# A two-layer encoder's feed-forward layer: weight sums by accumulating DMAs, a new order of seven products, and PSUM banks exchanged between two products

## Chip, cores and metric

The kernel runs on one core of a Trainium2 chip. The metric is the device time of one execution in microseconds (us). Shown are the median of three runs, and one profiled execution.

## What is computed

The reference is an encoder trunk with 1024 tokens of width 1024 and two layers. Each layer is a token mixer (latent attention in layer 0, differential attention in layer 1) and a gated feed-forward part, with a norm before and after each. The change lies in the feed-forward part alone:

```python
def conv_ffn(x, w_up, conv_w, conv_b, w_down):
    u = x @ w_up                                   # 1024 -> 2 * 2816
    c = conv_b
    for j in range(3):                             # width 3, along the tokens
        c = c + conv_w[j] * up[:, j:j + s]         # up: u padded by one token at both ends
    g, val = c[..., :2816], c[..., 2816:]
    return (gelu(g) * val) @ w_down                # 2816 -> 1024

h = h + rms_norm(conv_ffn(rms_norm(h, norm_g[i, 2]), ...), norm_g[i, 3])
```

## The kernel before, in words

All is fp32. Each operand of a matmul is split in a high part (rounded, by ScalarE, `split`, line 185) and the rest (a subtraction on VectorE, line 186); three matmuls (`mm3`, lines 176 and below) make one product of full precision. Both products of the feed-forward part are done by Strassen-Winograd: a 2x2 partition with seven block products in place of eight, at the cost of sums of operands and results.

**First product** (`Sums`, lines 882 to 935). HID = 2816 gives NC = 22 blocks n of 128 hidden columns, each with a gate and a value part. A block has seven products of 12 matmuls (128x128 by 128x512), named for their operands: `ae`, `bg`, `su`, `cd`, `ac`, `sh`, `dg`. They run in three PSUM accumulators: x (`ae`, then `bg` on top), y (`su`, then `ac`, then `dg` on top), z (`cd`, then `sh` on top). Between two products on one accumulator VectorE or ScalarE reads it: after `su` an add and a copy, after `ac` a copy and `add(q3, z, q3)`, after `sh` `add(q1, z, q1)` (line 931). y and z are the two halves of one two-bank PSUM tile (`big`, two buffers); x is a one-bank tile (`pv` or `pj` in turn). The loop over the blocks (lines 1081 to 1124) runs `ae(n)`, `su(n)`, `sh(n-1)`, `dg(n-1)`, `cd(n)`, `bg(n)`, `ac(n)`; the first four blocks have their `ae` and `bg` done ahead, so there the loop has five products. The weights and their sums come from SyncE's and GpSimd's DMA queues; two of the sums are made by accumulating DMAs (lines 856 and 857). `hidden` does the convolution and the gating, `left` the sums of the left operands of the second product, which go to DRAM (`sl_d`).

**Second product** (lines 973 to 1214). The 22 hidden blocks make G = 11 pairs g. With A, B the even and odd block for tokens 0 to 511, C, D those for tokens 512 to 1023, and e, f, g, h the quarters of the pair's rows of w_down, the seven products are, in order: A e; S4 h; B g; S1 (f - e); D (g - h + f - e); S2 (h - f + e); S3 (h - f). Each product is 11 operands times 4 token tiles times 3 matmuls of 512 columns, and accumulates in four PSUM banks: alternately `lone_banks` (the one-bank tiles pv, t, t, pj) and `pairs_of_banks` (two `big` tiles). S3 adds onto the banks of S2.

- `operands` (line 1006) splits, for each g, the left operand (loaded from `sl_d` in chunks of four g, `load_sr`, two buffers) and the right one, into a ring of five wide slots (`pairs`); the last product's eleven operands go to slots of their own (`drop=True`) and its matmuls run token tile by token tile.
- `load_q` (line 987) loads e by SyncE's queue and h, g, f by GpSimd's, one product ahead of use. The sums f - e and so on are subtractions on VectorE (`u`, lines 1031 and 349), in place in `raw[g]`, a wide slot of four quarters per pair.
- SBUF has 20 wide slots (2048 floats a partition) and 15 narrow ones.
- `finish_tile(t)` adds the residual and the norm for 128 tokens: tiles 0 to 3 behind S2, tiles 4 to 7 each behind its part of S3. In layer 0 `put` turns each tile for the next layer, and `ahead` loads and splits that layer's first weights (partly on GpSimd).

The instructions are put in order for each engine by a planner that models times; priorities follow the order of the program. DMAs stamped with one token (`then`, line 980) keep their order on GpSimd's queue. Waits between engines are derived from the tiles that are read and written. Each engine's queue runs in order.

Of the kernel before, what the change touches and what calls it, by code (L numbers as in the profile page):

```python
# [120 lines left out]
def hybrid_encoder_kernel(  # L121
# [697 lines left out]
    def ffn(i, aT, rest, first, res_ap, dst_ap, ahead):  # L819
# [8 lines left out]

        cw = cp.tile([P, 2 * NC * 4], F32, name="cw", tag="cw")
        nc.sync.dma_start(out=cw, in_=conv[i])  # L830

        taps = cw[:, NC * 4 :].rearrange("p (b j) -> p b j", j=4)[:, :, :3]
        nc.vector.tensor_scalar(out=taps, in0=taps, scalar1=-1.0, scalar2=None, op0=ALU.mult)
# [48 lines left out]
        class Sums:  # L882
# [16 lines left out]
            def ae(self, w):  # L899
                self.x = small(("pv", "pj")[self.n % 2])  # L900
                product(self.x, w, 0, "e")
                copy(self.m1, self.x)
# [5 lines left out]
            def open(self, w):  # L908
                if self.parked:
                    self.place()  # L910
                    copy(self.q[0], self.parked[1])
                self.w = w
                o = big()
                self.y, self.z = o[:, :512], o[:, 512:]
# [6 lines left out]
            def cd(self):  # L921
                product(self.z, self.w["s"], 0, "e-f")
# [51 lines left out]
        A, B_, S1, S2, S3, S4, D_ = 6, 4, 0, 1, 2, 3, 5  # L974
        E, F, G_, H = 0, 1, 2, 3
# [11 lines left out]
        def load_q(g, q):  # L987
            if g == len(raw):
                raw.append(ar.alloc(2048))
            src = w_down[i, 2 * g + q // 2][:, (q % 2) * 512 : (q % 2 + 1) * 512]  # L990
            if q == E:
                nc.sync.dma_start(out=rq(g, q), in_=src)
            else:
                then(nc.gpsimd.dma_start(out=rq(g, q), in_=src))  # L994

        def load_sr(at, g, n):
            sr = r_sr.next()
            then(
                nc.gpsimd.dma_start(  # L999
                    out=sr.f[:, : n * 512].rearrange("p (g t) -> p g t", g=n),  # L1000
                    in_=sl_d[g : g + n, :, at * 512 : (at + 1) * 512].rearrange("g p t -> p g t"),
                )
            )
            return sr

        def operands(at, right, ahead=None, drop=False, last=None, loaded=()):
# [5 lines left out]
            sr, loaded = None, list(loaded)  # L1012
            for g in range(G):
                if ahead is not None:
                    load_q(g, ahead)
                if last and g == G - 1:
                    src = last()
                else:
                    if g % 4 == 0:
                        sr = loaded.pop(0) if loaded else load_sr(at, g, min(4, G - g - (last is not None)))  # L1020
                    src = sr.f[:, (g % 4) * 512 : (g % 4 + 1) * 512]
# [4 lines left out]
                split(right(g), *w.cols(512, 512))  # L1026
# [3 lines left out]

        def u(g, op, a, b, q):
            op(rq(g, q), rq(g, a), rq(g, b))
            return rq(g, q)
# [26 lines left out]
        for m in range(2):  # L1060
            for n in range(2):
                sums[2 * m + n].ae(w1[2 * m + n])
# [18 lines left out]
        for n in range(NC):  # L1081
# [8 lines left out]
            if end:  # L1090
                aT.free("u")
                for g in range(2):
                    load_q(g, E)
# [7 lines left out]
            if n + 1 < NC:  # L1101
                nxt = weights(n + 1)
            cur.cd()
            if end:
                aT.free("e-f")
                for g in range(2, 4):
                    load_q(g, E)
            if n >= 4:
                cur.bg(w["ab"])
            if n == NC - 2:  # L1110
# [3 lines left out]
                loaded = [load_sr(A, 4 * j, 4) for j in range(2)]  # L1114
            if end:
                aT.free("g")
                for g in range(4, 6):
                    load_q(g, E)
            else:
                weights_late(nxt)  # L1120
            cur.ac()
            if end:
                aT.free("h-f")
            old, w = cur, nxt
# [4 lines left out]
        xb = lone_banks()  # L1129
        for g in times(xb, operands(A, lambda g: rq(g, E), H, False, lambda: hid[0][:, :512], loaded)):  # L1130
            if g == 1:
                cur.sh()
                aT.free("h")
                for g2 in range(6, G - 1):
                    load_q(g2, E)
            elif g == 3:
                cur.dg()
                aT.free("-u-g")
                load_q(G - 1, E)
# [8 lines left out]
        yb = pairs_of_banks()  # L1148
        product2(yb, operands(S4, lambda g: rq(g, H), G_))
# [4 lines left out]
        product2(xb, operands(B_, lambda g: rq(g, G_), F), True)  # L1154
# [4 lines left out]
        product2(yb, operands(S1, lambda g: u(g, sub, F, E, E)), True)  # L1159
# [38 lines left out]
        ops = list(operands(S3, lambda g: u(g, sub, H, F, E), drop=True))  # L1198
# [340 lines left out]
```

## Time and profile before

| | |
|---|---|
| median of 3 runs | 2652.86 us (2648.47 to 2655.63) |
| the profiled execution | 2651.43 us, of which its span from first to last instruction is 2649.7 us |
| TensorE busy | 2552.2 us, 96%; mean granted clock 0.988 of full speed |
| VectorE busy | 1958.5 us, 74% |
| ScalarE busy | 1341.4 us, 51% |
| GpSimd busy | 366.3 us, 14% |
| DMA | 313.33 MB, mean 118 GB/s |

PE is TensorE's matmul row and PEld its weight loads, DVE is VectorE, ACT ScalarE, POOL GpSimd, SP SyncE. A time in square brackets behind a group is the idle time of the engine just before it, with what ended it. The first layer's feed-forward products lie at about 600 to 1040 us (first) and 1037 to 1264 us (second), the second layer's at about 2000 to 2420 and 2418 to 2641 us.

### The profile page before, as it was taken

How to read it: one execution, taken by the hardware profiler on the slowest of the kernel's cores; microseconds unless marked ns; L12 is line 12 of the kernel's file. 1: busy time of each engine (PE TensorE's matmuls, PEld its weight loads, DVE VectorE, ACT ScalarE, POOL GpSimd, SP SyncE). 2: the span in 40 equal slices, each digit the busy share in tenths (PEclk: the TensorE clock that was granted, in tenths of full speed). 3: DMA queues.
4: the chain of work that ended last, by engine and by line, in shares of the span. 5: the costliest groups of instructions: out<-in, count | busy, mean ns of one | idle time of the engine just before them, and what ended most of it. 6: DMA issues, size and time to landing. Idle time of an engine off the chain costs nothing. (4 is left out here: it accounts for less than half of the span.)

```text
span 2649.7 us, 34107 instructions
## 1 busy us (share of the span) xinstructions
PE 2552.2 (96%) x12720; PEld 2124.2 (80%) x12720; DVE 1958.5 (74%) x3085; ACT 1341.4 (51%) x2411; POOL 366.3 (14%) x464
## 2 busy tenths in 40 slices
PE   8999999998999999999799999998998999999998
PEld 7888888786788888887588888887786888888886
DVE  6776666566877777678578787788677877777677
ACT  5454455445545545445355555566445554555444
POOL 0000001101111112200322222223001111112200
PEclk9999999999999999999899999999999999999999
DMA  4211102235445545633533222323235554546534
GB/s 157 67 43 40 36 32 85 80 131 155 147 133 146 151 143 180 225 122 112 155 80 80 65 71 70 80 64 120 102 119 151 152 146 132 147 142 212 198 112 147
DMA packets 123209, 313.33 MB, mean 118 GB/s; under 512 B 13473, under 2 KB 34849, under 8 KB 120225
## 3 DMA queue, kind: packets, MB, share of 16 engines
q0 software_dynamic: 49520, 154.17, 20.9%
q1 hardware_dynamic: 60592, 148.58, 16.4%
q10 hardware_dynamic: 12928, 8.39, 1.0%
q8 instruction: 100, 1.64, 0.3%
q14 instruction: 69, 0.56, 0.1%
HBM read 216.19 MB, written 69.73 MB: 108 GB/s over the span
## 5 line engine op out<-in xcount | busy, mean ns | idle before, releaser
L176 PE MATMUL big<-a,a 128*128 128x512 f32 (+2 forms) x3696 | 886.6, 388 | 20.5 <-ACT a L185 9.2
L176 PEld LDWEIGHTS big<-a,a 128*128 128x128 f32 x3696 | 680.4, 189 | 152.8 <-ACT a L185 11.5
L176 PE MATMUL pj<-a,a 128*128 128x512 f32 x1878 | 478.8, 396 | 9.1 <-DVE b L186 6.1
L176 PEld LDWEIGHTS pj<-a,a 128*128 128x128 f32 x1878 | 344.5, 189 | 82.4 <-DVE b L186 7.5
L176 PE MATMUL big<-a,b 128*128 128x512 f32 x1296 | 366.1, 404 | 13.7 <-DMA b<-b 5.8
L176 PE MATMUL pv<-a,a 128*128 128x256 f32 (+1 forms) x2130 | 365.1, 321 | 7.3 <-DVE a L186 4.7
L176 PEld LDWEIGHTS pv<-a,a 128*128 128x128 f32 x2130 | 315.6, 196 | 47.1 <-DVE a L186 11.4
L176 PEld LDWEIGHTS big<-a,b 128*128 128x128 f32 x1296 | 236.1, 189 | 75.0 <-DVE b L352 16.9
L185 ACT ACTIVATE a<-t 128x512 fp32r<-128x512 f32 (+1 forms) x376 | 206.5, 584 | 175.2 <-PE t L242 172.9
L186 DVE TENSOR_TENSOR a<-t,a 128x512 fp32r<-128x512 f32 (+1 forms) x376 | 239.9, 665 | 51.2 <-ACT a L185 50.6
L185 ACT ACTIVATE a<-a 128x512 fp32r<-128x512 f32 x306 | 175.7, 624 | 188.6 <-PE big L176 83.1
L185 ACT ACTIVATE a<-b 128x1024 fp32r<-128x1024 f32 (+2 forms) x198 | 203.9, 1034 | 106.1 <-PE big L176 42.9
L176 PE MATMUL big<-a 128*128 128x512 f32 x1056 | 244.9, 393 | 6.5 <-DVE b L352 6.5
L186 DVE TENSOR_TENSOR a<-a,a 128x512 fp32r<-128x512 f32 x306 | 196.6, 686 | 71.2 <-ACT a L185 71.2
L176 PEld LDWEIGHTS big<-a 128*128 128x128 f32 x1056 | 199.3, 189 | 49.6 <-DVE b L352 8.1
L186 DVE TENSOR_TENSOR a<-b,a 128x1024 fp32r<-128x1024 f32 (+5 forms) x178 | 211.7, 1192 | 29.6 <-ACT a L185 29.5
L242 PE MATMUL t<-ident,b 128*128 128x128 f32 x1456 | 205.2, 276 | 25.2 <-DVE a L186 10.2
L242 PEld LDWEIGHTS t<-ident,b 128*128 128x128 f32 x1456 | 169.4, 141 | 60.6 <-DVE a L186 19.3
L1404 ACT ACTIVATE b<-b,s 128x1024 f32<-128x1024 f32 x128 | 146.8, 1149 | 103.5 <-DVE s L1393 102.4
L1393 DVE CUSTOM_DVE_ANT_0 b<-big,a 128x1024 f32<-128x1024 f32 x128 | 154.1, 1216 | 23.5 <-PE big L176 22.0
L880 ACT ACTIVATE b<-big 128x512 f32<-128x512 f32 x132 | 77.9, 590 | 161.2 <-DVE big L352 110.6
L940 DVE SCALAR_TENSOR_TENSOR b<-b,cw,b 128x1023 f32<-128x1023 f32 x88 | 112.9, 1283 | 34.2 <-ACT b L939 34.2
(148 smaller groups left out, 2656.6 us busy)
## 6 DMA issues: line engine op xcount, KB each, us to landing
b<-w_up SPq DMA_DIRECT2D x132, 256.0 KB, 2.9
a<-sl_d POOLq DMA_DIRECT2D x28, 1024.0 KB, 5.5
b<-w_up SPq DMA_DIRECT2D x52, 512.0 KB, 3.4
b<-w_up POOLq DMA_DIRECT2D x88, 256.0 KB, 4.4
sl_d<-a POOLq DMA_DIRECT2D x22, 1024.0 KB, 7.0
a<-w_down POOLq DMA_DIRECT2D x66, 256.0 KB, 5.4
b<-b POOLq DMA_DIRECT2D x64, 256.0 KB, 3.8
h_d<-b SPq DMA_DIRECT2D x24, 512.0 KB, 2.8
```

Source lines behind the costliest of these rows:

```text
L176: return nc.tensor.matmul(o, lhsT=lhsT, rhs=rhs, start=start, stop=stop, skip_group_check=more)
L185: nc.scalar.activation(hi, src, AF.Copy)
L186: (eng or nc.vector).tensor_tensor(out=lo, in0=src, in1=hi.bitcast(F32), op=ALU.subtract)
L242: nc.tensor.transpose(t[:, j, :], c, ident)
L880: nc.scalar.activation(dst, src, AF.Copy)
L940: nc.vector.scalar_tensor_tensor(out=t[:, 1:], in0=e[:, : S - 1], scalar=wc[0], in1=t[:, 1:], op0=ALU.mult, op1=ALU.add)
L1393: nc.vector.tensor_tensor_reduce(out=em.f, in0=sc, in1=dv, scale=1.0, scalar=3.0e38, op0=ALU.add, op1=ALU.min, accum_out=s8[:, m : m + 1],)
L1404: nc.scalar.activation(em.f, em.f, AF.Exp, bias=s8[:, m : m + 1], scale=-1.0, accum_out=z)
```

## The change

- First product: y gets a one-bank tile `t` (two buffers), z the tile `pj`, x the tile `pv` (in the four blocks done ahead `pv` and `pj` as before). `bg(n)` now stands before `cd(n)`.
- Second product: it starts in `pairs_of_banks` and takes turns with `lone_banks` from there. The order of the last three products is now S2, D, S3 in place of D, S2, S3, so that S2 is still in the pairs of banks that S3 adds to, but D lies between them.
- Weight sums: odd hidden blocks are stored with the opposite sign (another set of conv taps and biases is negated at the start), and the right half of the result has its sign turned by the gain, so that every sum of weights has plus signs only: e, then + f, + h, + g in place in `raw[g]`'s first quarter, and h + f in its third. Each is an accumulating DMA from w_down on GpSimd's queue (`add_q`), issued behind the split of the same g. `raw[g]` has three quarters. The 44 subtractions a layer are gone; three products take their right operand with a minus sign (`neg`: the same two instructions in other forms).
- Chunks of left operands are requested when a chunk has been used up (`load_left`), in one list over all products; the e quarters are requested a little earlier.

```diff
-        taps = cw[:, NC * 4 :].rearrange("p (b j) -> p b j", j=4)[:, :, :3]
-        nc.vector.tensor_scalar(out=taps, in0=taps, scalar1=-1.0, scalar2=None, op0=ALU.mult)
+        taps = cw[:, NC * 4 :].rearrange("p (b s j) -> p b s j", s=2, j=4)
+        for part in (taps[:, :, 0, :3], taps[:, :, 1, 3:]):
+            nc.vector.tensor_scalar(out=part, in0=part, scalar1=-1.0, scalar2=None, op0=ALU.mult)
...
-            def ae(self, w):
-                self.x = small(("pv", "pj")[self.n % 2])
+            def ae(self, w, tag="pv"):
+                self.x = small(tag)
...
-                o = big()
-                self.y, self.z = o[:, :512], o[:, 512:]
+                self.y = small("t")
...
             def cd(self):
+                self.z = small("pj")
                 product(self.z, self.w["s"], 0, "e-f")
...
-        A, B_, S1, S2, S3, S4, D_ = 6, 4, 0, 1, 2, 3, 5
-        E, F, G_, H = 0, 1, 2, 3
+        S1, S2, S3, S4, B_, D_, A = range(7)
+        E, G_, H = 0, 1, 2
...
+        def weight(g, name):
+            q = "efgh".index(name)
+            return w_down[i, 2 * g + q // 2][:, (q % 2) * 512 : (q % 2 + 1) * 512]
+
+        def load_e(g):
+            raw.append(ar.alloc(1536))
+            nc.sync.dma_start(out=rq(g, E), in_=weight(g, "e"))
+
+        def load_q(g, q, name):
+            then(nc.gpsimd.dma_start(out=rq(g, q), in_=weight(g, name)))
+
+        def add_q(g, q, name):
+            then(nc.gpsimd.dma_start(out=rq(g, q), in_=weight(g, name), accum_op=ALU.add))
...
+        chunks = [(at, g, min(4, G - g - (at == A))) for at in (A, S4, B_, S1, S2, D_, S3) for g in range(0, G, 4)]
+        def load_left():
+            if chunks:
+                at, g, n = chunks.pop(0)
+                loaded.append(r_sr.next())
...
+        def operands(q, ahead=lambda g: None, neg=False, last=None, drop=False):
             for g in range(G):
...
                 split(src, *w.cols(0, 512))
-                split(right(g), *w.cols(512, 512))
+                hi, lo = w.cols(512, 512)
+                if neg:
+                    nc.scalar.activation(hi, rq(g, q), AF.Copy, scale=-1.0)
+                    minus_sum(lo, rq(g, q), hi.bitcast(F32))
+                else:
+                    split(rq(g, q), hi, lo)
+                if g % 4 == 3 or g == G - 1:
+                    loaded.pop(0)
+                    load_left()
+                ahead(g)
...
+            if n >= 4:
+                cur.bg(w["ab"])
...
             cur.cd()
...
-            if n >= 4:
-                cur.bg(w["ab"])
...
-        xb = lone_banks()
-        for g in times(xb, operands(A, lambda g: rq(g, E), H, False, lambda: hid[0][:, :512], loaded)):
+        xb = pairs_of_banks()
+        for g in times(xb, operands(E, lambda g: load_q(g, H, "h"), last=lambda: hid[0][:, :512])):
...
-        yb = pairs_of_banks()
-        product2(yb, operands(S4, lambda g: rq(g, H), G_))
+        yb = lone_banks()
+        product2(yb, operands(H, lambda g: load_q(g, G_, "g")))
...
-        product2(xb, operands(B_, lambda g: rq(g, G_), F), True)
+        product2(xb, operands(G_, lambda g: add_q(g, E, "f"), neg=True), True)
...
-        product2(yb, operands(S1, lambda g: u(g, sub, F, E, E)), True)
+        product2(yb, operands(E, lambda g: add_q(g, E, "h"), neg=True), True)
...
         nc.sync.dma_start(out=gp, in_=norm_g[i, 3].partition_broadcast(P))
+        nc.vector.tensor_scalar(out=gp[:, 512:], in0=gp[:, 512:], scalar1=-1.0, scalar2=None, op0=ALU.mult)
...
+        xb = pairs_of_banks()
+        product2(xb, operands(E, lambda g: add_q(g, E, "g")))
+        for t in range(4):
+            add(f[t].f[:, 512:], xb[t], f[t].f[:, 512:])
         yb = lone_banks()
-
-        def g_less_u(g):
-            u(g, sub, H, E, E)
-            return u(g, sub, G_, E, G_)
-
-        product2(yb, operands(D_, g_less_u))
+        product2(yb, operands(E, lambda g: add_q(g, H, "f"), neg=True))
         for t in range(4):
             add(f[4 + t].f[:, :512], yb[t], m1v[t])
         ar.free(m1)
-        xb = pairs_of_banks()
-        product2(xb, operands(S2, lambda g: rq(g, E)))
-        for t in range(4):
-            add(f[t].f[:, 512:], xb[t], f[t].f[:, 512:])
...
-        ops = list(operands(S3, lambda g: u(g, sub, H, F, E), drop=True))
+        ops = list(operands(H, drop=True))
```

## Rows read from the trace of the kernel before

**Rows 1.** The page's busy times: engine, us, share, instructions.

```profile
PE 2552.2 (96%) x12720; PEld 2124.2 (80%) x12720; DVE 1958.5 (74%) x3085; ACT 1341.4 (51%) x2411; POOL 366.3 (14%) x464
```

**Rows 2.** Timeline of PE around S3, both layers: start, us, instructions, [idle before].

```profile
1226.43 13.02 PE L176 MATMUL big<-a 128*128 128x512 f32 x56 [1.77 <-DVE b L352]
...
1253.04 2.61 PE L176 MATMUL big<-a 128*128 128x512 f32 x7 [2.03 <-DVE b L352]
...
2607.95 16.87 PE L176 MATMUL big<-a 128*128 128x512 f32 x66 [1.78 <-DVE b L352]
2625.68 15.26 PE L176 MATMUL big<-a 128*128 128x512 f32 x66 [0.86 <-DVE b L352]
```

**Rows 3.** Timeline of PE in the first product, blocks with seven products.

```profile
706.35 2.88 PE L176 MATMUL pv<-a,a 128*128 128x512 f32 x12
709.07 2.88 PE L176 MATMUL big<-a,a 128*128 128x512 f32 x12
...
720.89 3.04 PE L176 MATMUL big<-a,b 128*128 128x512 f32 x12
...
772.21 6.51 PE L176 MATMUL big<-a,a 128*128 128x512 f32 x28
...
1009.37 3.06 PE L176 MATMUL big<-a,b 128*128 128x512 f32 x12
```

**Rows 4.** Groups of weight loads, 720.89 to 1009.37 us: count, busy, mean ns, idle before.

```profile
L176 PEld LDWEIGHTS big<-a,b 128*128 128x128 f32 x180 | 32.6, 188 | 11.0 <-DVE b L352 4.5
```

**Rows 5.** Timeline of PE at the first product's start and end.

```profile
647.83 3.01 PE L176 MATMUL big<-a,a 128*128 128x512 f32 x12 [1.94 <-DVE b L352]
652.43 1.20 PE L176 MATMUL big<-a,a 128*128 128x512 f32 x4 [1.59 <-ACT b L880]
653.81 3.06 PE L176 MATMUL big<-a,b 128*128 128x512 f32 x12 [0.18 <-DVE b L352]
...
671.05 3.02 PE L176 MATMUL big<-a,b 128*128 128x512 f32 x12 [1.30 <-DVE b L352]
...
1029.43 3.02 PE L176 MATMUL big<-a,b 128*128 128x512 f32 x12 [0.66 <-DVE b L352]
...
2035.61 4.60 PE L176 MATMUL big<-a,b 128*128 128x512 f32 x12 [0.18 <-DVE b L352]
```

**Rows 6.** Timeline of DVE at four places of the first product.

```profile
644.13 1.42 DVE L352 TENSOR_TENSOR b<-b,b 128x512 f32<-128x512 f32 x2 [4.21 <-DMA b<-w_up]
...
653.07 0.68 DVE L352 TENSOR_TENSOR b<-big,b 128x512 f32<-128x512 f32 x1
...
777.85 0.69 DVE L352 TENSOR_TENSOR b<-big,b 128x512 f32<-128x512 f32 x1 [1.95 <-PE big L176]
...
1028.70 0.68 DVE L352 TENSOR_TENSOR b<-big,b 128x512 f32<-128x512 f32 x1
```

**Rows 7.** Groups of the second product, 1074.9 to 1226.4 us: the weight sums.

```profile
L349 DVE TENSOR_TENSOR a<-a 128x512 f32<-128x512 f32 x44 | 29.9, 690 | 11.1 <-DMA a<-w_down 10.1
```

**Rows 8.** One line's instructions, duration ns min/median/max: the form that the signed split takes.

```profile
L356 DVE SCALAR_TENSOR_TENSOR b<-b,b x16: 679/682/693, 582.7 to 2013.9; 128x512 f32<-128x512 f32 x16
```

**Rows 9.** One line's instructions: an accumulating DMA on POOL, its issue and its landing.

```profile
L856 POOL DMA_DIRECT2D b<-w_up x44: 843/859/943, 617.9 to 2377.5; - x44
...
DMA to landing us min/median/max: 3.5/4.1/4.8
```

**Rows 10.** One line's instructions: issue and landing of the left operands' chunks.

```profile
L999 POOL DMA_DIRECT2D a<-sl_d x42: 712/756/790, 1020.0 to 2596.1; - x42
...
DMA to landing us min/median/max: 4.5/5.4/8.2
```

**Rows 11.** Stretch by engine (busy us, count), granted clock, DMA share and GB/s.

```profile
2607.90:2612.00 4.10, 4.05 (x12) 3.20 (x13) 4.10 (x7) 3.56 (x11) 0.00 (x0) 0.64 0.37 94
```

**Rows 12.** Timeline of ACT and DVE: splits of S3's operands in the second layer.

```profile
2600.52 6.88 ACT L185 ACTIVATE a<-a 128x512 fp32r<-128x512 f32 x13 [3.48 <-DMA a<-sl_d]
...
2601.18 5.51 DVE L186 TENSOR_TENSOR a<-a,a 128x512 fp32r<-128x512 f32 x9 [1.80 <-ACT a L185]
...
2619.79 2.49 DVE L186 TENSOR_TENSOR a<-a,a 128x512 fp32r<-128x512 f32 x4
```

**Rows 13.** Timeline of PE behind the first layer's S3.

```profile
1270.73 0.79 PE L176 MATMUL big<-a,a 128*128 128x512 f32 x1 [6.52 <-ACT a L185]
```

More of the change, by code (lines that the diff above doesn't have):

```diff
@@ L985, in rq @@
             return raw[g].f[:, q * 512 : (q + 1) * 512]
[L987 to L1001, printed above, removed]
-                )
-            )
-            return sr
@@ L1006, in operands @@
-        def operands(at, right, ahead=None, drop=False, last=None, loaded=()):
-            sr, loaded = None, list(loaded)
+        def weight(g, name):
[6 more added lines that the diff above has]
+            then(nc.gpsimd.dma_start(out=rq(g, q), in_=weight(g, name)))
@@ new lines, in add_q @@
+        def add_q(g, q, name):
+            then(nc.gpsimd.dma_start(out=rq(g, q), in_=weight(g, name), accum_op=ALU.add))
+        chunks = [(at, g, min(4, G - g - (at == A))) for at in (A, S4, B_, S1, S2, D_, S3) for g in range(0, G, 4)]
+        loaded = []
+        def load_left():
+            if chunks:
+                at, g, n = chunks.pop(0)
+                loaded.append(r_sr.next())
+                then(
+                    nc.gpsimd.dma_start(
+                        out=loaded[-1].f[:, : n * 512].rearrange("p (g t) -> p g t", g=n),
+                        in_=sl_d[g : g + n, :, at * 512 : (at + 1) * 512].rearrange("g p t -> p g t"),
+                    )
+                )
@@ L1013, in operands @@
+        def operands(q, ahead=lambda g: None, neg=False, last=None, drop=False):
             for g in range(G):
-                if ahead is not None:
-                    load_q(g, ahead)
+                src = loaded[0].f[:, (g % 4) * 512 : (g % 4 + 1) * 512]
                 if last and g == G - 1:
                     src = last()
[L1018 to L1021, printed above, removed]
@@ L1029, in operands @@
                 yield w
-        def u(g, op, a, b, q):
-            op(rq(g, q), rq(g, a), rq(g, b))
-            return rq(g, q)
         def times(banks, ops, more=False):
@@ L1061, in ffn @@
             for n in range(2):
-                sums[2 * m + n].ae(w1[2 * m + n])
+                sums[2 * m + n].ae(w1[2 * m + n], ("pv", "pj")[n])
             for n in range(2):
@@ L1092, in ffn @@
                 for g in range(2):
-                    load_q(g, E)
+                    load_e(g)
             if old:
@@ L1102, in ffn @@
                 nxt = weights(n + 1)
+            if n >= 4:
+                cur.bg(w["ab"])
+            if end:
+                aT.free("g")
+                for g in range(2, 4):
+                    load_e(g)
             cur.cd()
@@ L1105, in ffn @@
                 aT.free("e-f")
-                for g in range(2, 4):
-                    load_q(g, E)
-            if n >= 4:
-                cur.bg(w["ab"])
+                for g in range(4, 6):
+                    load_e(g)
             if n == NC - 2:
@@ L1113, in ffn @@
                 aT.free("e")
[L1114 to L1119, printed above, removed]
+                load_left()
+                load_left()
+            if not end:
                 weights_late(nxt)
@@ L1123, in ffn @@
                 aT.free("h-f")
+                for g in range(6, 8):
+                    load_e(g)
             old, w = cur, nxt
@@ L1133, in ffn @@
                 aT.free("h")
-                for g2 in range(6, G - 1):
-                    load_q(g2, E)
+                for g2 in range(8, G - 1):
+                    load_e(g2)
             elif g == 3:
@@ L1138, in ffn @@
                 aT.free("-u-g")
-                load_q(G - 1, E)
+                load_e(G - 1)
                 finish_block(cur)
```

## Prediction

> **What bounds the kernel now.** I read the busy times first: TensorE is busy for 96% of the span, VectorE for 74% [rows 1]. So a part of the change gains only where TensorE stands still or runs slow today, and the next view is the timeline of PE through both feed-forward products. In the second product there is no gap from one operand to the next, nor from one product to the next, until S3: there PE waits 1.77 us in the first layer and 1.78 us in the second for VectorE's reads of S2's banks, since S3 adds onto them, and later once more (2.03 and 0.86 us) [rows 2]. Behind the 1.78 us the granted clock is 0.64 for 4 us, a mean of full speed and the lower of TensorE's two levels, 1.2 of 2.4 GHz [rows 11]; 66 matmuls take 16.87 us there and 15.26 us next [rows 2]. In the first product an ordinary group of 12 starts 2.72 us before the next (706.35 to 709.07), so the seven groups of a block should take 19.04 us. But from the `dg` at 720.89 to that at 1009.37 us there are 15 blocks, 19.23 us each: 0.19 us are lost in each [rows 3]. The groups of weight loads say where: those of `dg`, the only ones whose weights lie in a narrow slot, are the only ones with a named wait, 4.5 us in 15 blocks, for an add on VectorE [rows 4]. At the ends the same wait is plain: `dg` starts at 653.81 and 1029.43 us, and the adds at 653.07 and 1028.70 us, 0.68 us long, end just before [rows 5, 6]. That add reads z, and `dg` writes y. They are different banks, but halves of one tile, so the wait comes from the tile and not from the data. (That is my reading; its opposite is the second rival.)
>
> **The change, part by part.** The sum is made against the profiled execution's own 2651.43 us; the median of the runs stands 1.43 us above it.
>
> *Weight sums.* 44 subtractions a layer, 29.9 us of VectorE, go away [rows 7]. PE has no wait on them, so they are worth 0 by themselves. In their place come 44 accumulating DMAs and 22 plain ones on GpSimd's queue, where 33 plain ones were. An accumulating one costs 0.86 us of GpSimd, and lands in 4.1 us, at most 4.8 [rows 9]; per operand of 12 matmuls (2.72 us) GpSimd has one, and a quarter of a left chunk (0.76 us [rows 10]): about 1.05 us of 2.72. Each waits for the split of its g, and behind it on GpSimd's queue stands the next chunk of left operands, but that chunk needs the same splits to free its buffer. The sum is wanted one product later, 11 operands x 2.72 = 29.9 us less the ring's five operands (13.6 us), so 16.3 us are there for at most 0.86 + 8.2 us (the worst landing of a chunk [rows 10]). Cost 0, covered by the product between. If the cover were gone, PE would wait out what lies above 16.3 us; no row comes near.
>
> *Signed splits.* 33 a layer in another form: 682 ns at the median against 690 for a subtraction [rows 7, 8]. 0. The two conv-tap instructions and the turned gain are one short VectorE instruction each; the gain must wait for a load issued just behind S1, and four operands that are split by then cover 10.9 us. 0.
>
> *y and z in tiles of their own.* The wait of `dg` goes: 17 blocks with the small loss in each layer, 34 x 0.19 = **-6.5 us**. At the end of the first product 0.66 us in each layer [rows 5], the second within 0.05 us: **-1.3 us**. In the first blocks, where only five products run, the waits at 652.43 (for a copy of y, while z is to be written), 653.81 and 671.05 are of this kind: 3.07 us [rows 5], in the second layer 3.00, and there 12 matmuls take 4.60 us in place of 3.06 behind them [rows 5]: 7.6 us in all. These blocks also wait for weights (VectorE stands 4.21 us for a sum that comes by DMA [rows 6]), which the change leaves as it is. So between 0 and -7.6; I take half, **-3.8 us**.
>
> *z in a single bank.* `cd(n)` must now wait for the add that reads z behind `sh(n-1)`. In a full block `dg` and `bg` lie between, 5.44 us. The row to size it by: `sh` ends 24 x 0.227 us into the 28 matmuls at 772.21, at 777.65, and the add ends at 778.54, 0.9 us later [rows 3, 6]. So 0. In blocks 1 to 3 only `dg` lies between, 2.72 us, and there the add is later: `sh` ends 2.72 us behind 647.83, the add at 653.75, 3.2 us later [rows 5, 6]. That is 0.5 us, for six such blocks 0 to 3 us; y's bank also comes out of the ring of the last transposes. Together **+1.0 us**.
>
> The Trainium skill's Perfetto Trace Analysis (Matmul Optimizations) wants all eight PSUM banks used, so that reads overlap the next matmuls, and this change takes the first product from six banks to four. No row of the kernel before shows the four; by the rule the sum would not be a gain but the third rival's loss.
>
> *Order of S2, D, S3.* S2's banks are read while D runs, so S3 does not wait for them: **-3.55 us**, and the slow clock behind the second of these gaps, 16.87 - 15.26 = **-1.6 us**. What is late next is S3's operands. They need eleven wide slots, and at D the 20 are full: 11 raw, 5 in the ring, 2 chunks, the gains, and m1, which D's sums read. The first that comes free is the ring's, when PE is done with D's seventh operand, 4 x 2.72 = 10.9 us before D's end; from there each split frees a raw slot. 22 splits at 0.61 us each (5.51 us for nine [rows 12]) take 13.5 us, and end 2.6 us into S3, whose first pass reads the last operand 6.8 us in. The third left chunk is asked for when four operands are split (5.2 us), and lands 0.76 + 5.4 us later [rows 10], 0.5 us into S3; its three operands take 4 us, so 4.5 us against 5.4. Covered with 1 us to spare, gone if it lands 8.2 us late; S3's operands wait for that chunk today too, 3.48 us [rows 12]. I take **+0.5 us a layer, +1.0**, with 0 and +17 as ends (the first rival).
>
> *Behind S3.* With D between, token tiles 0 to 3 can be finished during D and leave VectorE to tiles 4 to 7. The later waits in S3 (2.03, 0.86) stay, being between the two halves of one tile. PE stands 6.52 us behind the first layer's S3, for a split on ScalarE [rows 13]; that may shrink by 0 to 6. Since the planner's order there is not visible, I take **-1.5 us**.
>
> Sum: -6.5 - 1.3 - 3.8 + 1.0 - 3.55 - 1.6 + 1.0 - 1.5 = -16.25. 2651.43 - 16.25 = 2635.2, and 1.4 more for the median: **2636.6 us**, -0.6%. A measurement of this kernel tells about 0.3%, 8 us, from no change.
>
> **The rivals.**
>
> *S3's operands come too late (0.15; ends slower).* Place: the first matmuls of S3 in both layers. If no slot is free before D ends, four operands take 5.2 us, the chunk 6.2, the last three 4: the last is there 15.3 us into S3 where it is wanted at 6.8. That is 8.5 us a layer, 17 in all. It decides once the first split of S3 starts later than some 9 us before D's end. The gains of the first product stay (-10.6), the gap's 3.55 too, nothing behind S3 is won, and the clock falls in both layers (+1.6): +4.5, 2657 us, with the late landing of 8.2 us 2663. For it speaks that the slots are just full; against it that the ring's slots come free four operands early.
>
> *The add is not what `dg` waits for, or the wait moves to `cd` (0.15).* Then the first product is as before, and -3.55 - 1.6 + 1.0 - 1.5 = -5.7 is left: 2647 us. For it speaks that the wait is only inferred from two times that meet; against it that they meet at all three places.
>
> *Four banks bind in the first product (0.04; slower).* With z's read in no cover, each of 42 blocks would lose the 0.9 us from `sh`'s end to the add's: +38, and with -5.7 from the rest 2685 us. It decides where the planner sets the add over 5.4 us late. Against it: the same block's convolution needs that add, so it comes early on VectorE.
>
> **How the numbers follow.** Forecast 0.6, the three rivals 0.34, and 0.06 for an order of the planner that I don't foresee. In the forecast the ends of its own terms (first blocks -7.6 to 0, behind S3 -6 to 0, z 0 to 3) give 2626 to 2645. The range takes in the second rival and the nearer ones of the first: 2626 to 2654. Faster by over 0.3% (below 2644.9): nearly all of the forecast and a little of the rest, 0.62. Slower by over 0.3% (above 2660.8): the upper part of the first rival, the third, and a third of the unforeseen, 0.12. The rest, 0.26, is within.
>
> **What would show it.** Right: blocks of 19.05 us in the first product, `dg` with no named wait; no gap of PE at the start of S3; VectorE some 30 us a layer less busy in the second product. Wrong: blocks still at 19.2 us, with the wait now at `cd`; PE waiting at S3's start for a split or for a left chunk; a right operand's split waiting for w_down's DMA.

## The result, and the profile after

The changed kernel takes 2674.5 us (median of 4 runs, 2673.5 to 2676.2) beside 2651.8 us (median of 4 too) for the kernel before on the same chip: a ratio of 1.0086, interval 1.0068 to 1.0103. It is slower by 23 us, where 16 us faster were forecast. The page's busy times (they answer to [rows 1]) and its line on GpSimd's DMA queue (packets, MB, share of 16 DMA engines; before: 49520, 154.17 MB, 20.9%):

```profile
PE 2559.7 (96%) x12720; PEld 2134.6 (80%) x12720; DVE 1895.4 (71%) x3001; ACT 1345.4 (50%) x2411; POOL 431.5 (16%) x530
...
q0 software_dynamic: 60432, 171.47, 25.6%
```

VectorE has 63 us less to do, as meant, and nothing was won by it. Where did the time go? The GELU of the first and last block of each first product marks the way:

| start of the GELU, us | first, layer 0 | last, layer 0 | first, layer 1 | last, layer 1 | span |
|---|---|---|---|---|---|
| before | 661.3 | 1053.1 | 2043.7 | 2434.6 | 2649.7 |
| after | 664.9 | 1052.1 | 2047.7 | 2439.1 | 2672.9 |

Two things are seen. From the last mark to the end, where the second layer's second product lies, 18.7 us are lost; the first layer loses 5 between its last mark and the next layer's first. And of the 11.6 us forecast for y and z in tiles of their own next to nothing is left: the way from the first mark to the last of a layer is 387.2 and 391.4 us, where it was 391.8 and 390.9.

The timeline of PE around S3, both layers (it answers to [rows 2, 13]):

```profile
1226.40 0.50 PE L176 MATMUL big<-a 128*128 128x512 f32 x1 [2.78 <-ACT a L185]
1228.49 1.65 PE L176 MATMUL big<-a 128*128 128x512 f32 x3 [1.59 <-DVE a L186]
1231.02 3.78 PE L176 MATMUL big<-a 128*128 128x512 f32 x8 [0.87 <-DVE a L186]
1238.35 8.27 PE L176 MATMUL big<-a 128*128 128x512 f32 x24 [3.55 <-ACT a L185]
1248.39 3.49 PE L176 MATMUL big<-a 128*128 128x512 f32 x14 [1.76 <-DVE a L186]
1252.29 3.26 PE L176 MATMUL big<-a 128*128 128x512 f32 x13 [0.41 <-DVE a L186]
...
1278.19 2.11 PE L176 MATMUL big<-a,a 128*128 128x512 f32 x8 [1.31 <-DVE rs_r L205]
...
2614.61 0.50 PE L176 MATMUL big<-a 128*128 128x512 f32 x1 [3.95 <-ACT a L185]
2616.61 5.06 PE L176 MATMUL big<-a 128*128 128x512 f32 x11 [1.50 <-DVE a L186]
2628.33 3.74 PE L176 MATMUL big<-a 128*128 128x512 f32 x7 [6.66 <-ACT a L185]
2633.94 21.20 PE L176 MATMUL big<-a 128*128 128x512 f32 x80 [1.87 <-DVE a L186]
```

S2's banks stop nobody any more, but S3 waits for its operands' splits, 11.0 us in the first layer and 14.0 in the second (the sums of the idle times in brackets). The 6.52 us behind S3 [rows 13] have shrunk to 1.31. The splits wait in turn; the table of waits (us in all, times, longest) names for what:

```profile
POOL a L1001 <- issue: 92.7, 41, 7.1
...
ACT a L185 <- DMA a<-sl_d: 65.8, 13, 11.6
...
POOL a L1012 <- issue: 35.3, 12, 5.5
```

L1012 is the chunks' load, L1001 the accumulating DMA. ACT waited 20.2 us for chunks before. The chunks themselves are little slower, 6.0 us from issue to landing against 5.4 [rows 10]: they are asked for late. GpSimd's timeline in D's product, which starts at 1193.5 us:

```profile
1201.10 0.79 POOL L1012 DMA_DIRECT2D a<-sl_d  x1 [1.82 <-DVE rs_r L205]
1202.88 0.88 POOL L1001 DMA_DIRECT2D a<-w_down  x1 [1.00 <-issue]
1204.18 0.88 POOL L1001 DMA_DIRECT2D a<-w_down  x1 [0.42 <-issue]
1208.67 0.87 POOL L1001 DMA_DIRECT2D a<-w_down  x1 [3.61 <-issue]
1209.90 0.85 POOL L1001 DMA_DIRECT2D a<-w_down  x1 [0.36 <-issue]
1216.40 0.79 POOL L1012 DMA_DIRECT2D a<-sl_d  x1 [5.65 <-DVE rs_r L205]
1217.58 0.85 POOL L1001 DMA_DIRECT2D a<-w_down  x1 [0.39 <-issue]
1225.33 1.76 POOL L1001 DMA_DIRECT2D a<-w_down  x2 [6.90 <-issue]
```

S3's first chunk goes out at 1216.40, 22.9 us into D's product; before the change it went out 10 us into the product ahead of S3. Its buffer had long been free: the last split that read the chunk before it in that buffer is this one on VectorE, and it ends at 1205.5 us.

```profile
1204.83 0.69 DVE L186 TENSOR_TENSOR a<-a,a 128x512 fp32r<-128x512 f32 x1
```

In the 10.9 us from there GpSimd issues two adds and stands for the rest. It stands for "issue", that is for nothing that the profile names, and longest one or two adds behind a chunk (3.61 and 6.90 us). The 5.65 us right before the chunk are put down to `rs_r`, a tile of the norm that the chunk does not use, so that name is no cause either. The stretches of D and S3 (busy us and counts by engine, granted clock, DMA share, GB/s), first before, then after:

```profile
1194.00:1224.00 30.00, 30.00 (x134) 24.86 (x133) 25.88 (x43) 17.97 (x33) 2.27 (x3) 1.00 0.30 106
1224.00:1256.00 32.00, 28.19 (x128) 22.54 (x128) 29.33 (x50) 13.86 (x36) 0.00 (x0) 0.97 0.28 99
```

```profile
1194.00:1224.00 30.00, 29.62 (x131) 24.21 (x129) 20.10 (x36) 14.62 (x33) 8.51 (x10) 1.00 0.90 221
1224.00:1256.00 32.00, 21.41 (x69) 15.33 (x70) 23.69 (x43) 16.15 (x35) 4.21 (x5) 0.73 0.65 186
```

The DMA engines go from 0.30 to 0.90 busy, and PE, which waits, has a mean granted clock of 0.73 in S3's stretch, between full speed and the lower level of 0.5. So there were two suspects (GpSimd's queue, the DMA engines) and a third that these traces don't rule out: the new order, with eleven operands wanted at once.

In the first product VectorE waits for a DMA that it hardly waited for before. Over the whole kernel these waits were 18.5 us and are 93.0. From 2080 to 2400 us, in layer 1, there was none (in the same part of layer 0 there was one, of 1.4 us), and now:

```profile
DVE b L352 <- DMA b<-w_up: 45.0, 16, 4.8
...
PE pj L176 <- DVE b L352: 5.0, 5, 1.6
```

Its timeline in layer 1 shows what stands behind that wait, up to the add that reads z (`b<-pj,b`); `sh` then writes z, 1.06 us late:

```profile
2114.94 0.69 DVE L352 TENSOR_TENSOR b<-b,b 128x512 f32<-128x512 f32 x1 [4.33 <-DMA b<-w_up]
2115.55 1.22 DVE L958 TENSOR_TENSOR b<-b,b 128x1024 f32<-128x1024 f32 x1
2116.69 1.22 DVE L186 TENSOR_TENSOR a<-b,a 128x1024 fp32r<-128x1024 f32 x1
2117.82 0.68 DVE L349 TENSOR_TENSOR a<-b 128x512 f32<-128x512 f32 x1
2118.43 1.22 DVE L186 TENSOR_TENSOR a<-b,a 128x1024 fp32r<-128x1024 f32 x1
2119.56 0.68 DVE L352 TENSOR_TENSOR b<-pj,b 128x512 f32<-128x512 f32 x1
```

```profile
2120.30 3.03 PE L176 MATMUL pj<-a,a 128*128 128x512 f32 x12 [1.06 <-DVE b L352]
```

In such a block of the kernel before, z's add (`b<-big,b`) came first, and the sums only behind it:

```profile
2152.11 0.68 DVE L352 TENSOR_TENSOR b<-big,b 128x512 f32<-128x512 f32 x1
2152.71 0.68 DVE L349 TENSOR_TENSOR a<-b 128x512 f32<-128x512 f32 x1
2153.30 1.41 DVE L352 TENSOR_TENSOR b<-b,b 128x512 f32<-128x512 f32 x2
```

The longest waits of the first product stand in its first blocks. `dg` (`t<-a,b`) writes y, and waits for ScalarE's copy out of it, 4.66 us in layer 0 and 4.54 in layer 1; the 12 matmuls behind it take 4.02 us in place of 2.88, at a mean granted clock of 0.83 from 662 to 672 us. ScalarE comes to that copy (`b<-t`, L882) late, behind a split that waits for w_up's DMA, and the GELU. First PE, then ScalarE:

```profile
666.53 1.73 PE L176 MATMUL t<-a,b 128*128 128x512 f32 x4 [4.66 <-ACT b L882]
668.06 4.02 PE L176 MATMUL pj<-a,a 128*128 128x512 f32 x12
```

```profile
662.57 1.06 ACT L185 ACTIVATE a<-b 128x1024 fp32r<-128x1024 f32 x1 [3.57 <-DMA b<-w_up]
663.64 1.28 ACT L953 ACT_TABLE_LOAD   x1
664.93 1.06 ACT L953 ACTIVATE b<-b 128x1024 f32<-128x1024 f32 x1
665.90 0.58 ACT L882 ACTIVATE b<-t 128x512 f32<-128x512 f32 x1
```

### The profile page after: what moved, and what is told of

The parts are those of the page before. It is cut to its first block, busy times and chain, and to the rows that moved or that the text cites. A ratio compares the mean times of both kernels' runs of the same rounds, so it can differ in the third digit from the quotient of the medians.

```text
span 2672.9 us, 34277 instructions
## 1 busy us (share of the span) xinstructions
PE 2559.7 (96%) x12720; PEld 2134.6 (80%) x12720; DVE 1895.4 (71%) x3001; ACT 1345.4 (50%) x2411; POOL 431.5 (16%) x530
## 3 DMA queue, kind: packets, MB, share of 16 engines
q0 software_dynamic: 60432, 171.47, 25.6%
## 4 chain that ended last, share of the span: by engine, by line
PE 56%; DMA 9%; DVE 8%; issue 7%; ACT 3%; POOL 1%; POOLq 0%; DVEq 0%; SPq 0%; ACTq 0%
PE pj L176 16%; PE big L176 16%; PE t L176 11%; PE pv L176 10%; DMA b<-w_up 6%; DVE a L186 2%; PE t L242 2%; ACT a L185 1%; DMA a<-sl_d 1%; DVE b L352 1%; DMA a<-w_down 1%; DVE b L1403 1%; DVE rstd L199 1%; DVE b L958 1%; ACT b L1414 0%
## 5 line engine op out<-in xcount | busy, mean ns | idle before, releaser
L176 PE MATMUL pj<-a,a 128*128 128x512 f32 x2502 | 637.1, 397 | 15.2 <-DVE b L186 6.1
L176 PEld LDWEIGHTS pj<-a,a 128*128 128x128 f32 x2502 | 464.4, 190 | 119.8 <-DVE b L352 12.3
L176 PE MATMUL pv<-a,a 128*128 128x256 f32 (+1 forms) x2562 | 467.4, 331 | 7.1 <-DVE a L186 4.4
L176 PEld LDWEIGHTS pv<-a,a 128*128 128x128 f32 x2562 | 395.5, 193 | 63.3 <-DVE a L186 10.5
L176 PE MATMUL big<-a,a 128*128 128x512 f32 (+2 forms) x1584 | 382.6, 383 | 5.9 <-ACT a L185 2.7
L176 PEld LDWEIGHTS big<-a,a 128*128 128x128 f32 x1584 | 284.1, 191 | 51.1 <-ACT a L185 4.4
L176 PE MATMUL t<-a,a 128*128 128x512 f32 x1056 | 253.6, 390 | 0.0
L176 PE MATMUL big<-a,b 128*128 128x512 f32 x768 | 231.7, 405 | 10.1 <-issue 6.3
L176 PEld LDWEIGHTS t<-a,a 128*128 128x128 f32 x1056 | 199.3, 189 | 41.8
L882 ACT ACTIVATE b<-t 128x512 f32<-128x512 f32 x132 | 78.1, 591 | 196.5 <-DVE t L352 126.7
```

Source lines behind the costliest of these rows:

```text
L176: return nc.tensor.matmul(o, lhsT=lhsT, rhs=rhs, start=start, stop=stop, skip_group_check=more)
L882: nc.scalar.activation(dst, src, AF.Copy)
```

## Experiments

Fourteen kernels; ratios are to the kernel before, with their interval.

### Which part of the second product costs the time

**VectorE's sums.** Banks and order stay; f is loaded into a fourth quarter, and VectorE adds.

```diff
-product2(xb, operands(G_, lambda g: add_q(g, E, "f"), neg=True), True)
+product2(xb, operands(G_, lambda g: load_q(g, F, "f"), neg=True), True)
-product2(yb, operands(E, lambda g: add_q(g, E, "h"), neg=True), True)
+product2(yb, operands(E, neg=True, plus=F), True)
...
+                if plus is not None:
+                    add(rq(g, q), rq(g, q), rq(g, plus))
```

> The weight sums go back to VectorE (22 plain loads of f a layer, 88 adds in place of 88 accumulating DMAs); banks and order of the products stay as in the changed kernel. Theory (POOL's queue and the DMA engines, loaded by the accumulating DMAs, bring the left chunks late): ACT's waits for a<-sl_d fall from 65.8 us to about the 20 us of before, PE's waits for ACT L185 and DVE L186 (19.6 and 8.7 us) to under 5, and the time to 2646 to 2652. Rival (the new order of the products, S3 right behind D with its eleven operands asked for late, is the cause whoever makes the sums): PE's waits stay over 20 us and the time over 2666.

2640.5 us, 0.995 (0.9936 to 0.9965). The waits for chunks:

```profile
ACT a L185 <- DMA a<-sl_d: 10.1, 4, 3.6
```

PE's waits at S3 are 1.3 us in layer 0 and 1.3 in layer 1. So the accumulating DMAs cost 34 us (36 by the two ratios), and the rest of the change wins 13. The order of the products is not to blame, nor are the slots that rival one counted, which are the same here. The GELU marks of this kernel are 665.9, 1055.9, 2035.2 and 2426.9 us, and its span 2639.1: beside the kernel before, 11.3 us are won between the layers and 2.9 behind the last mark, where S2, D and S3 lie, and 3.6 are lost in and ahead of the first products.

**Plain loads in their place.**

```diff
-then(nc.gpsimd.dma_start(out=rq(g, q), in_=weight(g, name), accum_op=ALU.add))
+then(nc.gpsimd.dma_start(out=rq(g, q), in_=weight(g, name)))
```

> The 88 accumulating DMAs become 88 plain loads of the same bytes to the same places on the same queue; the weight sums are left out. If the adding itself is what the DMA engines spend their time on: DMA share of the windows 1164 to 1224 falls from 0.9 to under 0.6, chunks land in time, and the time is 2648 to 2656. If it is only that so many DMAs stand in POOL's queue: share and POOL's issue waits (92.7 us on that line) stay, and the time stays at 2668 to 2676.

2644.3 us, 0.9966 (0.9957 to 0.9976), for a kernel that leaves the weight sums out: the same bytes on the same queue without the adding cost 4 us beside VectorE's sums, not 34. One line's instructions, then GpSimd's queue on the page:

```profile
L1001 POOL DMA_DIRECT2D a<-w_down x88: 539/539/574, 1095.6 to 2591.9; - x88
...
  issue: 17.3, 8
```

```profile
q0 software_dynamic: 54800, 171.47, 23.0%
```

The issue takes 0.54 us in place of 0.87, and the issue waits on this line are 17.3 us in place of 92.7; on this line and the chunks' together they are 41.6 in place of 128.0. The DMA share in 1164 to 1224 us falls only to 0.72 and 0.73 (from 0.91 and 0.90), above what was expected, with the chunks in time.

**The chunks on SyncE's queue.**

```diff
-                then(
-                    nc.gpsimd.dma_start(
+                chunk_then(
+                    nc.sync.dma_start(
                         out=loaded[-1].f[:, : n * 512]...
```

> The left chunks are requested on SP's queue instead of POOL's, the accumulating DMAs stay. Theory with the weight on POOL's order (a chunk's request stands behind adds that wait to issue): chunks are requested when their slot comes free, S3's PE waits fall under 8 us in all, time 2650 to 2660. Theory with the weight on the DMA engines (0.9 busy): the request comes earlier but its data no sooner, landing grows over 8 us, time over 2666.

2654.6 us, 1.0005 (0.9995 to 1.0015): 20 us come back with every accumulating DMA kept. The DMA share is 1.01 in 1194 to 1224 us, more than in the changed kernel, and yet:

```profile
POOL a L1005 <- issue: 69.3, 42, 6.6
...
ACT a L185 <- DMA a<-sl_d: 19.5, 6, 4.7
```

GpSimd still stands, but no chunk stands behind it. It was the queue, not full DMA engines, that held the chunks up. PE's waits at S3 did not fall as far as expected (under 8 us): 3.4 us are left in layer 1, but 12.2 in layer 0, the longest 8.6 for an add on VectorE between two token tiles. Why VectorE is late there was not settled.

**f alone by DMA; no adds in D.** Two doses. In the first VectorE adds h and g (44 accumulating DMAs, none in D's product); the second leaves f's add onto h out, and with it that part of S3's right operand.

```diff
...
-product2(xb, operands(E, lambda g: add_q(g, E, "g")))
+product2(xb, operands(E, lambda g: add_q(g, H, "f"), plus=H))
...
```

```diff
-product2(yb, operands(E, lambda g: add_q(g, H, "f"), neg=True))
+product2(yb, operands(E, neg=True))
```

> f is added by accumulating DMAs (22 a layer, to e during B*g and to h during S2's product), h and g by VectorE: 44 accumulating DMAs in place of 88, none of them in H*h, S1's or D's product. Theory (what makes the chunks late is the backlog on POOL's queue, which now has two products' time to drain before S3's chunks): ACT's waits for a<-sl_d 20 to 30 us, time 2640 to 2650. Rival (any accumulating DMAs between the chunks bring them late): waits over 45 us, time over 2660.

> The accumulating DMAs that stand in POOL's queue during D's product (f onto h, 11 a layer) are left out, and with them that part of S3's right operand; the 33 others of a layer stay. If the backlog of the three products before D is what holds S3's chunks up: little is won, time 2666 to 2674. If it is the adds right ahead of S3's chunks: S3's waits are gone, time 2644 to 2654. I expect the second for the most part, as each chunk waits for the adds just ahead of it.

2643.9 us, 0.9961 (0.9948 to 0.9975), with 25.7 us of waits for chunks; and 2650.7 us, 0.9994 (0.9983 to 1.0004), with 44.9. Leaving out the 22 adds in D's products alone brings 24 of the 34 us: what counts most is what stands on the queue right ahead of S3's chunks.

**Chunks in one row.** The left factors lie in DRAM so that a chunk is 128 rows of 8 KB, not 512 of 2 KB. The blocks' stores into them change with it, to rows of 2 KB.

```diff
-out=loaded[-1].f[:, : n * 512].rearrange("p (g t) -> p g t", g=n),
-in_=sl_d[g : g + n, :, at * 512 : (at + 1) * 512].rearrange("g p t -> p g t"),
+out=loaded[-1].f[:, : n * 512],
+in_=sl_d[at][:, g * 512 : (g + n) * 512],
...
```

> The changed kernel, its accumulating DMAs kept, but the left factors lie in DRAM so that a chunk is one row of 8 KB a partition (128 rows) instead of four rows of 2 KB (512 rows); the blocks' stores are of 2 KB rows instead. Theory A (POOL can have only so many rows under way: it stands longest, up to 6.9 us, one or two adds behind a chunk, until that chunk has landed): POOL's issue waits, 92.7 and 35.3 us, fall under 50 in all, S3's operands come in time, time 2645 to 2656. Theory B (the adds' own work on the DMA engines is what fills them, a chunk's rows are no matter): issue waits stay over 100 us, time 2666 or more.

2654.7 us, 1.0004 (0.9995 to 1.0014): 20 us by this layout, with every accumulating DMA kept. (The trace is of the fastest of the ten runs, 2646.4 us.)

```profile
POOL a L1003 <- issue: 50.8, 30, 5.8
...
ACT a L185 <- DMA a<-sl_d: 24.1, 9, 7.0
...
POOL a L1014 <- issue: 11.3, 3, 5.0
```

The issue waits fall from 128.0 to 62.1 us, above the 50 that theory A gave, while the DMA share in D's product rises to 1.01. So the rows of the chunks matter to GpSimd; that there is a fixed number of rows that may be under way was not shown, and the run with the chunks on SyncE's queue says that adds alone make it stand too (69.3 us).

**The old order with the new banks**, sums by VectorE: D's product on the single banks, before S2's.

```diff
-product2(xb, operands(E, plus=H))
-product2(yb, operands(E, neg=True, plus=G_))
+product2(yb, operands(G_, neg=True, plus=E, first=g_sum))   # g_sum: e += h
+product2(xb, operands(E))
...
```

> The kernel with VectorE's sums, but D's product ahead of S2's as before the change; the banks stay, so D's product (single banks) must wait for S1's sums to be read out of the same banks. Theory (the new order is worth the covered read-outs at S2's end, and it gives D's start a free pair): PE waits of 2 to 5 us a layer at D's start, S3's first operands as late as before the change; time 2646 to 2654. Rival (the order is worth nothing by itself, the 13 us come from the first product): within 2 us of 2640.5.

2660.1 us, 1.0021 (1.0012 to 1.003), 6 us beyond what was expected. The gaps at S3 are back (1.97 and 2.00 us in layer 0, and 4.46 behind it), and 1.9 us at D's start. With these banks, the order is worth 20 us. Not all of that is a gain over the kernel before, which had no wait at D's start: beside it, VectorE's sums win 14.2 us in this part.

### Why the first product won nothing

Three attempts at z's wait came first. In the changed kernel, z in the double tiles (only the last block in `pj`); on VectorE's sums, the third weights' split behind `ac`, and the five loads ahead of the convolutions:

```diff
-self.z = small("pj")
+self.z = small("pj") if self.n == NC - 1 else big()[:, :512]
```

```diff
-            if not end:
-                weights_late(nxt)
             cur.ac()
+            if not end:
+                weights_late(nxt)
```

```diff
+            if n + 1 < NC:
+                raw_next = weights_load(n + 1)
+            if old:
                 finish_block(old)
...
```

> First product alone: z goes to the two double buffers (which stand empty there) in all blocks but the last, in place of the one single bank. Theory: PE's waits pj <- DVE L352 (5.9 us, 8 times, 5 of them in layer 2) are gone and nothing takes their place: 5 to 6 us less than the changed kernel, about 2669. Rival: the late add behind them is VectorE's being behind, and the wait moves to the next reader of VectorE's or ACT's work (t or pv): under 2 us gained, 2673.

> The kernel with VectorE's sums, and in the first product the split of the next block's third weights is emitted behind the block's last product instead of ahead of it, so that VectorE's add that reads z (z is written again by the next block's product with h) stands before that split. Theory (z's wait is VectorE's queue: it stood idle for w_up's accumulating DMA, up to 4.8 us, and then had some 5 us of work to do before that add): PE's waits pj <- DVE L352, 9.2 us in 17 times, fall by 1.2 us each, to under 3 us, time 2633 to 2637. Rival (the wait is the DMA's own lateness, whatever stands behind it): the waits stay at 7 us or more, time 2639 to 2642.

> The kernel with VectorE's sums, and in the first product the five loads of the next block's weights are emitted ahead of the finished block's convolutions instead of behind them. Theory (VectorE, in order, stands for w_up's accumulating DMA, 43 and 45 us a layer in 16 waits, because that DMA is issued late, behind VectorE's convolutions, and z's add comes late behind it): those waits fall under 15 us a layer, PE's waits pj <- DVE L352 under 3 us, time 2632 to 2637. Rival (the loads are issued when their slot comes free, wherever they are emitted): waits and time as in the kernel with VectorE's sums, 2639 to 2642.

2682.3 us, 1.0114 (1.0092 to 1.0136); 2640.8, 0.9946 (0.9933 to 0.9958); 2642.4, 0.9956 (0.9941 to 0.9971). All three miss. z's wait stays (5.4 us in 7 times from 2080 to 2440 us with the double tiles; 12.7 and 10.8 us in all with the others), and so do VectorE's for w_up. So what makes it is neither the bank nor the place of the split or of the loads in the program. Why z in the double tiles is 8 us slower was not settled; its waits for chunks are 76.1 us in place of 65.8, and its trace is of the slowest of its four runs. The loads ahead and the chunks in one row, together, on VectorE's sums:

> VectorE's sums, the loads emitted earlier in the first product, and the chunks in one row a partition, all together. If each is worth what is expected of it alone: 2630 to 2636. If the rows only matter beside accumulating DMAs, as the run of VectorE's sums has POOL's issue waits at 9.4 and 9.2 us: the same as the loads emitted earlier alone, within 2 us.

2643.4 us, 0.9965 (0.9953 to 0.9976): without accumulating DMAs the rows don't matter.

What was left is VectorE's order. Before the change the sum of the next s weights (which waits for w_up's accumulating DMA) stood just behind z's add; in the changed kernel the planner put it five instructions ahead (the six rows above). The edit marks both with one token, as `then` does for DMAs, and so holds them in the order of before:

```diff
-add(s1[:, 512:], s1[:, :512], wg[:, :512])
+z_first(add(s1[:, 512:], s1[:, :512], wg[:, :512]))
...
-add(self.q[3], self.z, self.q[3])
+z_first(add(self.q[3], self.z, self.q[3]))   # z_first stamps one token
```

> The kernel with VectorE's sums, and in the first product VectorE's add that reads z is held ahead of the sum of the next s weights, which waits for w_up's accumulating DMA: the order that VectorE had before the change, and lost in it. Theory (that sum stands five instructions ahead of z's add in the changed kernel and makes VectorE wait 40 to 50 us a layer): DVE's waits for w_up fall under 5 us a layer, PE's waits pj <- DVE L352 from 9.2 us to under 2, time 2630 to 2636. Rival (PE runs at the pace at which the s weights come, and a later sum makes its split late instead): PE waits for L185 or L186 on t, time 2639 or more.

> The changed kernel with nothing but that order held on VectorE in the first product; accumulating DMAs and chunks as in the change. Theory: the first product comes 4 to 8 us shorter over both layers, S3's waits stay: 2666 to 2671. Rival (as S3's waits hang on how the DMAs of the second product meet, what is won ahead is lost there): 2672 to 2682.

> The changed kernel, all its accumulating DMAs kept, with the chunks in one row a partition and the order of z's add held. Theory (the accumulating DMAs cost what they do through POOL's room alone): as fast as VectorE's sums with the same order, within 4 us of that run. Rival (they cost time in other places too): 8 us or more behind it, as the chunks in one row were 14 us behind VectorE's sums.

| us, median | planner's order | order held |
|---|---|---|
| the changed kernel | 2674.5 | 2656.4, 1.0011 (1.0001 to 1.0022) |
| chunks in one row | 2654.7 | 2628.4, 0.99 (0.9881 to 0.9918) |
| VectorE's sums | 2640.5 | 2612.5, 0.9845 (0.9827 to 0.9864) |

Holding this order is worth 18 to 28 us, over twice what was expected. In the changed kernel with the order held, VectorE's waits for w_up are 7.0 us in all, and it reaches z's add with no wait and does the sums behind it:

```profile
2105.62 1.22 DVE L186 TENSOR_TENSOR a<-b,a 128x1024 fp32r<-128x1024 f32 x1
2106.75 0.68 DVE L352 TENSOR_TENSOR b<-pj,b 128x512 f32<-128x512 f32 x1
2107.36 1.40 DVE L352 TENSOR_TENSOR b<-b,b 128x512 f32<-128x512 f32 x2
```

By the starts of `dg`, the blocks from the fifth on take 19.04 us each here, but for the last. In the changed kernel about every other one does, and those between take up to 20.9; together they lose 3.0 us in layer 0 and 7.3 in layer 1. More comes from the first blocks: PE's two waits for the copy of y, 9.2 us, are gone. ScalarE's order changed with VectorE's there: in layer 0 it makes that copy at 660.4 us, and no split that waits for a DMA stands ahead of it. So the edit moved more than the one add. The way from the first to the last GELU is 385.1 us in both layers, and the first GELU comes at 659.1 us in place of 664.9, the last one of layer 1 at 2423.9 in place of 2439.1. S3's waits stay, as expected (PE's for ScalarE's splits are 21.6 us in all, 19.6 in the change). The last kernel of the table beats both: banks, order of the products and signs of the change, sums on VectorE, z's add ahead. With the adds on the DMAs and the chunks in one row the kernel is still 16 us behind it: PE's waits for the two splits are not gone (6.8 and 6.9 us in the whole kernel, beside 2.7 and 2.2), and its waits for chunks are 39.1 us beside 11.5.

## Why the prediction was wrong

- **Weight sums, "Cost 0, covered by the product between": the step that failed.** It cost 34 us by the run of VectorE's sums. The issue was sized right (0.87 us against 0.86 [rows 9]) and no split waited for a sum. What was not priced is the queue: I argued that a chunk behind an add "needs the same splits to free its buffer" and let the add's place on the queue go at its issue time, 1.05 us in 2.72. But GpSimd stood another 128 us before those two lines, so a chunk went out 10.9 us after its buffer was free, and the rows named in the prediction hold no instance of it. The trace of before had one: w_down's plain loads waited 36.5 us in 13 times for "issue", and the chunks 7.7 us.
- **S3's operands, +0.5 us a layer.** 11.0 and 14.0 us. That is the outcome of the first rival (8.5 us a layer, 2657 to 2663), and the trace that I named for it (PE waiting for a split, the split for a chunk) is the one that came. Its mechanism was another: the slots were no matter, since VectorE's sums use the same ones without a wait.
- **y and z in tiles of their own, -11.6 in all.** The reading of [rows 3, 4] was right: with the order held the blocks take 19.04 us, and the ways from first to last GELU shrink by 6.7 and 5.8 us. The first blocks, for which the sum took half of 7.6 us, win more than all of it: from the last product on `pj` that is done ahead to the fourth `dg` they take 68.0 us in place of 75.3 in layer 0, and 67.9 in place of 74.1 in layer 1. In the changed kernel all this was taken back by the planner's order on VectorE and ScalarE (75.1 us for the first blocks of layer 0), for which the prediction had 0.06. The second rival (wait not removed) is refuted.
- **z in a single bank, +1.0.** With the order held and z in its single bank no block loses anything, so the bank costs nothing. The wait in the changed kernel lies at `sh`, not at `cd`, for the add behind `ac`. The third rival had such a mechanism (an add that the planner sets late), with the wrong add and 38 us.
- The Trainium skill's Perfetto Trace Analysis (Matmul Optimizations) would have all eight banks in use; the fastest kernel here has four in the first product, and its blocks lose nothing. The runs don't bear the rule out for this loop.
- **S2, D, S3, -3.55 and -1.6.** Right in kind: no gap for S2's banks. **Behind S3, -1.5**: 5.2 us in layer 0 (6.52 to 1.31), within the ends given. The part was undersized: VectorE's sums win 14.2 us between the layers and at the end, where these terms and the +1.0 give 5.65.
- The weight sums alone put the time outside the range, 2626 to 2654: with them on VectorE it is 2640.5, inside, while with only the order held it is 2656.4, still outside. That 2640.5 lies 4 us from the forecast is luck: the first product won nothing, and the second won over twice what was summed.

## What to carry to other kernels

A DMA costs its queue more than its issue: on an in-order queue, look for what stands behind it and when that is wanted, and for waits that the profile calls "issue". Work that is free on an engine that is not the bound (VectorE's 63 us) was not worth moving to a queue that feeds the bound. When a change touches the order of the program, compare the order on every engine before and after: one instruction that waits for a DMA, set five places too early on VectorE, and what moved with it on ScalarE, cost as much as the change was to win.

## What the runs showed of the hardware

An accumulating DMA of 256 KB takes GpSimd 0.87 us to issue against 0.54 for a plain one. On the DMA engines the changed kernel's GpSimd queue takes 0.256 x 16 x 2672.9 = 10,950 engine-us, with plain loads of the same bytes 0.230 x 16 x 2645.4 = 9,735: 13.8 more for each of the 88. The mean of 256 KB on that queue of the second kernel is 14.9; it still holds the first product's 88 accumulating DMAs, and if these cost 13.8 more each too, a copy takes 13.0. So, as an estimate, an add takes 1.9 to 2.1 times a copy. The Trainium skill's Collectives: The Full Stack (The bandwidth ceiling) says that the adding step of a reduce-scatter reads two sources and so needs two read descriptors for each piece, where a copy needs one, and gives 1.93 as the measured ratio of the two collectives' rates. The estimate agrees with that, and so do the packets, 60432 against 54800: 64 more for each of the 88 DMAs.

How long GpSimd stands for "issue" on the lines of the adds and the chunks depended on the adding (41.6 us without it, 128.0 with it) and on the layout of the chunks on the queue (62.1 us with 128 rows, 128.0 with 512). The Trainium skill's DMA: Bandwidth & Descriptors (SWDGE vs HWDGE vs iDMA) says that GpSimd writes its descriptors to rings in SBUF, from which the engines drain them. That GpSimd stands when a ring is full would fit, but no run here shows the ring itself. With the DMA engines 1.01 busy in D's product, the kernels with the chunks on SyncE's queue and with the chunks in one row had PE busy without a gap there: full DMA engines were not by themselves what held S3 up.
